# Moving the matmul operands of a two-layer decoder step to other byte offsets in SBUF

## The chip, the cores and the metric

The kernel runs on one core of one Trainium2 chip. The metric is the device time of one execution in microseconds (us). Before the change it is 2714.65 us, the median of three runs that lie between 2712.93 and 2714.92 us.

## The reference

One inference step of a decoder with two layers, for 256 prompt tokens and 64 sample tokens together (320 token columns), with 2048 model features and a hidden width of 8192. Layer 0 mixes tokens by gated linear attention, layer 1 by a spatial gate; both are followed by a dense MLP with a squared ReLU.

```python
def sq_relu_mlp(x, w1, w2):
    return jnp.square(jax.nn.relu(x @ w1)) @ w2
...
            if i % N_MIXERS == 0:
                h, s = gla_mixer(x, gla_w_in[j], gla_w_gate[j], gla_b_gate[j], gla_norm_g[j],
                                 gla_w_out[j], gla_state0[j])
...
                h, v_rows = sg_mixer(x, sg_w_in[j], sg_b_in[j], sg_v_norm_g[j], sg_v_norm_b[j],
                                     sg_w_spatial[j], sg_b_spatial[j], sg_w_out[j])
...
            x = layer_norm(DEEPNORM_ALPHA * x + h, ln1_g[i], ln1_b[i])
            x = layer_norm(DEEPNORM_ALPHA * x + sq_relu_mlp(x, mlp_w1[i], mlp_w2[i]), ln2_g[i], ln2_b[i])
```

Nearly all of the arithmetic lies in the dense products `x @ w` of these five weight matrices and the two MLPs.

## The kernel before

Activations lie transposed: 16 blocks of 128 features, each 128 partitions by 320 tokens in fp32. A product is made of *units*: 4 x 128 rows by 256 columns of a weight matrix, 512 KB, loaded by one DMA of the SP queue (`unit`, line 126). ScalarE rounds the raw weights to a high part `wh` in fp32r (line 139), and VectorE makes the low part `wl` as the difference (line 140). Activations are kept as a high and a low part in the same way (`xh`/`xl`, `yh`/`yl`, `hh`/`hl` and so on, made by `parts`). A product of full precision is then three matmuls, written by `mm3` (lines 150 to 152): low weights by high activations, high weights by low activations, high weights by high activations. We call these three a **triple**. Each of its matmuls has a weight block of 128x128 as the stationary operand, and 320 token columns as the moving one. A unit is 8 triples; 16 triples that run over the 16 feature blocks fill one tile of 128 output features in PSUM.

After a normalization the first two units' columns are multiplied from the un-normalized values, with two more columns for the scale and the shift (the width is TW = 322 there, tiles `dgh` and `dgl`), while the normalization runs beside it (`gemm_of`); there are three such places of 64 triples each. All the other triples are 320 wide.

The weight parts live in rings: a `Ring` is a pool tag for `wh` and one for `wl`, with four buffers each. In the first layer's mixer there is one ring (`a`), after it two (`a` and `b`) in turn, so that a buffer comes back after 4 units first and after 8 units later. Tile's scheduler sets the order of the instructions of each engine; buffers that come free release the splitting of the next weights.

What matters here are **addresses inside a partition**, taken modulo 256 bytes. In the built program before the change:

- `wh` starts at 0. A block inside it starts at a multiple of 512 bytes, so every high block is at 0. `Ring.part` puts a gap of 16 words between the two tags, so every `wl` block is at 64.
- `bigtile` starts an activation tile of 320 columns at `LINE // 2` = 32 words. A feature block is 1280 bytes, five times 256, so every moving operand of a 320-wide triple, high or low, is at 128.
- A block of 322 columns is 1288 bytes, so in the 322-wide triples the moving operand of feature block k is at 8 k, and goes from 0 to 120. High and low parts are at the same offset there.

So before the change each of the 320-wide triples has the same three pairs of offsets (moving, stationary): (128, 64), (128, 0), (128, 0).

Of the kernel before, what the change touches and what calls it, by code (L numbers as in the profile page):

```python
# [8 lines left out]
F32 = mybir.dt.float32  # L9
F32R = mybir.dt.float32r  # L10
# [5 lines left out]
P = 128  # L16
D = 2048
KT = D // P
TP = 256
DB, DS = 8, 8  # L20
T = TP + DB * DS
# [12 lines left out]
LINE = 64  # L34
BIG = KT * T + LINE


V_BG, V_NG = 0, 8
V_L1G, V_L1B, V_L2G, V_L2B = 24, 56, 88, 120
V_SB, V_SG, V_SBB = 152, 184, 200  # L40
# [3 lines left out]
class Ring:  # L44


    def __init__(self, pool, tag):
        self.pool, self.tag, self.gap = pool, tag, False

    def part(self, p, name):  # L50

        t = self.pool.tile([P, UK, UN], F32R, tag=p + self.tag, name=name)
        if not self.gap:
            self.pool.tile([P, LINE // 4], F32, tag="gap", name=name + "_gap", bufs=1)
            self.gap = True
        return t


# [18 lines left out]
def step_kernel(ctx: ExitStack, tc: tile.TileContext, A):  # L77
# [3 lines left out]
    def nm(s):  # L81
        uid[0] += 1
        return f"{s}_{uid[0]}"
# [2 lines left out]
    cp = ctx.enter_context(tc.tile_pool(name="cp", bufs=1))  # L86
    big = ctx.enter_context(tc.tile_pool(name="big", bufs=1))
    wraw = ctx.enter_context(tc.tile_pool(name="wraw", bufs=3))
    wa = ctx.enter_context(tc.tile_pool(name="wa", bufs=4))
    mm = ctx.enter_context(tc.tile_pool(name="mm", bufs=4, space=bass.MemoryType.PSUM))  # L90
    gls = ExitStack()
    gl = gls.enter_context(tc.tile_pool(name="gl", bufs=4, space=bass.MemoryType.PSUM))
    mx = None

    rings = [Ring(wa, "a")]
    turn = [0]
    banks = [0]
    units = [0]
# [25 lines left out]
    def col(c):  # L124
        return vec[:, c : c + 1]
# [28 lines left out]
    def group(w, row0, cols, rh, rl, evict, side=None, width=T, before=None):  # L154

        ps = [mmtile(width) for _ in range(2 * len(cols))]
        for q in range(NU):
            if before is not None:
                before(q)
            for i, c in enumerate(cols):  # L160
                wh, wl = unit(w, row0, q, c, next_ring())
                for n in range(2):
                    for kk in range(UK):
                        k = q * UK + kk
                        mm3(ps[2 * i + n][:], wh, wl, kk, n, rh, rl, k, 0, width, k == 0, k == KT - 1)
                if side is not None:
                    side()
        for n in range(2 * len(cols)):
            evict(n, ps[n])
# [11 lines left out]
    lp = l2 = z = None  # L181
# [2 lines left out]
    w_in = A["gla_w_in"]  # L184
    C_Q, C_K, C_V, C_R = 0, H * DK, 2 * H * DK, 2 * H * DK + H * DV

    def bigtile(tag, dt, name, width=T):

        t = (lp if tag == "b1" else big).tile([P, BIG], dt, tag=tag, name=nm(name))
        start = LINE // 2 if width == T else 0
        return t[:, start : start + KT * width].rearrange("p (k t) -> p k t", t=width)

    def parts(pair, name, width=T):
        return bigtile(pair + "0", F32R, name + "h", width), bigtile(pair + "1", F32R, name + "l", width)

    xh, xl = parts("a", "x")
    o_all = bigtile("b0", F32, "o_all")  # L200

    gst = ExitStack()
# [104 lines left out]
    class Head:  # L307


        def __init__(hd, h):  # L310
            hd.h = h
            hd.eb, hd.ei, hd.ee = {}, {}, {}
# [304 lines left out]


    oh, ol = parts("a", "o")

    def split_o(ks):
        for k in ks:
            nc.scalar.copy(oh[:, k, 0:T], o_all[:, k, 0:T])
            nc.vector.tensor_sub(ol[:, k, 0:T], o_all[:, k, 0:T], oh[:, k, 0:T].bitcast(F32))

    def second_half():

        nonlocal lp, l2, z, gl, mx
        side.flush()
        split_o(range(4 * (H - 1), 4 * H))  # L630
        gst.close()
        gls.close()
        gl = ctx.enter_context(tc.tile_pool(name="gs", bufs=2, space=bass.MemoryType.PSUM))
        mx = ctx.enter_context(tc.tile_pool(name="mx", bufs=2, space=bass.MemoryType.PSUM))
        banks[0] = 3
        lp = ctx.enter_context(tc.tile_pool(name="lp", bufs=1))
        l2 = ctx.enter_context(tc.tile_pool(name="l2", bufs=2))
        wb = ctx.enter_context(tc.tile_pool(name="wb", bufs=4))
        rings.append(Ring(wb, "b"))
        wb.tile([P, LINE // 4], F32, tag="fill", name="fill_b", bufs=1)  # L640
        z = lp.tile([P, KT, T], F32, tag="z", name="z")
        lp.tile([P, 3 * LINE // 4], F32, tag="fill", name="fill_l")
        for q in range(2):
            nc.gpsimd.dma_start(z[:, 8 * q : 8 * q + 8, :], xT[:, 8 * q : 8 * q + 8, :])

# [112 lines left out]
    def gemm(w, row0, col0, rh, rl, evict, quad=False, side=None, before=None):  # L758

        i = 0  # L760
        while i < D // UN:
            n2 = 2 if quad and i == 0 else 1
            group(w, row0, [col0 + (i + m) * UN for m in range(n2)], rh, rl,
                  lambda n, ps, i=i: evict(2 * i + n, ps), side, before=before if i == 0 else None)
            i += n2

    def gemm_of(norm, out, w, col0, evict_raw, evict):

        yh, yl = parts(out, "y")
        norm.close()  # L770
        side = Side([lambda j=j: norm.apply(j, yh, yl) for j in range(KT)], 3 * NU)
        group(w, 0, (col0, col0 + UN), *norm.raw, evict_raw, side, width=TW)
        side.flush()
        for i in range(2, D // UN):
            group(w, 0, (col0 + i * UN,), yh, yl, lambda n, ps, i=i: evict(2 * i + n, ps))
        return yh, yl
# [23 lines left out]
    def mlp(i, norm, y_in, h_in, vg, vb, raw, last=False):  # L800

        w1, w2 = A["mlp_w1"][i], A["mlp_w2"][i]
        NC_ = 4
        for c in range(NC_):
            hs = []

            def sq_relu(j, x, r):
                if not hs:
                    hs.extend(parts(h_in, "h"))
                hh, hl = hs  # L810
                f = l2.tile([P, T], F32, tag="f", name=nm("f"))
                nc.vector.scalar_tensor_tensor(f[:], x, 0.0, r[:], op0=ALU.max, op1=ALU.mult)
                nc.scalar.copy(hh[:, j, 0:T], f[:])  # L813
                nc.vector.tensor_sub(hl[:, j, 0:T], f[:], hh[:, j, 0:T].bitcast(F32))  # L814

            def evict(j, ps):
                r = l2.tile([P, T], F32, tag="r", name=nm("r"))
                nc.scalar.activation(r[:], ps[:], AF.Relu)
                sq_relu(j, ps[:], r)

            def evict_raw(j, ps):
                t, wb_ = norm.correct(ps)
                r = l2.tile([P, T], F32, tag="r", name=nm("r"))
                nc.scalar.activation(r[:], t[:], AF.Relu, bias=wb_)
                sq_relu(j, r[:], r)

            if c == 0:
                yh, yl = gemm_of(norm, y_in, w1, 0, evict_raw, evict)
            else:
                gemm(w1, 0, c * D, yh, yl, evict)  # L830
            if c < NC_ - 1:
                def evz(j, ps, s=ALPHA if c == 0 else 1.0):
                    nc.vector.scalar_tensor_tensor(z[:, j, :], z[:, j, :], s, ps[:], op0=ALU.mult, op1=ALU.add)
                gemm(w2, c * D, 0, *hs, evz)
            else:
                return residual_gemm(w2, *hs, c * D, 1.0, vg, vb, raw, last=last)
# [4 lines left out]
    def before(q):  # L841
        if q == NU - 1:
            second_half()

    norm = residual_gemm(A["gla_w_out"], oh, ol, 0, ALPHA, V_L1G, V_L1B, "b", quad=True,
                         side=side, before=before)
    norm = mlp(0, norm, "a", "b", V_L2G, V_L2B, "a")


# [21 lines left out]
    def put_v(j, x, bias):  # L871
        nonlocal v, nv
        if j == 0:
            v = bigtile("a0", F32, "v")
            nv = Norm(v, V_SG, V_SBB)
        vj = v[:, j, 0:T]
        nc.scalar.activation(vj, x, AF.Gelu, bias=bias)
        if j >= KT // 2:
            nc.vector.tensor_sub(vj, vj, nv.c[:])
        nv.add(j)  # L880
        if j == 3:
            spatial()

    def ev_v_raw(j, ps):
# [2 lines left out]
        nc.vector.tensor_add(bias[:], wb_, col(V_SB + KT + j))  # L887
        put_v(j, t[:], bias[:])

    yh, yl = gemm_of(norm, "b", A["sg_w_in"], D, ev_v_raw, lambda j, ps: put_v(j, ps[:], col(V_SB + KT + j)))  # L890

    nv.close()
    oV = A["o_vT"].rearrange("(k p) t -> p k t", p=P)
# [39 lines left out]
        steps.append(lambda j=j: mixed(j, *mix(j)))  # L933
    side = Side(steps, 6 * NU)
    gemm(A["sg_w_in"], 0, 0, yh, yl, ev_u, side=side)
    ph, pl = parts("b", "p")
    for k in range(KT):
        nc.scalar.copy(ph[:, k, 0:T], v[:, k, 0:T])  # L938
        nc.vector.tensor_sub(pl[:, k, 0:T], v[:, k, 0:T], ph[:, k, 0:T].bitcast(F32))

    norm = residual_gemm(A["sg_w_out"], ph, pl, 0, ALPHA, V_L1G + KT, V_L1B + KT, "a", quad=True)
    norm = mlp(1, norm, "b", "a", V_L2G + KT, V_L2B + KT, "b", last=True)


    on_pool = (5, 9, 13)
    dh, dl = norm.raw
    ps = {}
# [17 lines left out]
    for j in range(KT):  # L965
        y, g, b = z[:, j, :], col(norm.vg + j), col(norm.vb + j)
# [79 lines left out]
```

## Time and profile before

| What | Value |
|---|---|
| median of three runs | 2714.65 us |
| the profiled execution: its own time | 2714.89 us |
| the profiled execution: its span, first to last instruction | 2713.2 us |
| granted TensorE clock, mean over the span | 0.999 |
| HBM read, written | 409.6 MB, 22.0 MB |
| share of the DMA engines' time in the queue of the weights | 47.8% |

The profile is one execution. Its own time is 1.7 us longer than its span, and 0.24 us longer than the median. In the rows that follow, a group is named by source line, engine, operation and by the program's tile names, out<-in. "PE" is a matmul and "PEld" a weight load; matmuls overlap in the pipeline, so that the duration of one is about twice the distance to the next one.

### The profile page before, as it was taken

Reading aid. Unit: us, or ns where it says so; the run is one execution under the profiler, and the core shown is the slowest. Engines: PE = TensorE matmul, PEld = TensorE weight load, DVE = VectorE, ACT = ScalarE, POOL = GpSimd, SP = SyncE. Lnnn points to the kernel's source line nnn. Section 1 sums busy time; section 2 is a strip of 40 time slices with the busy share of each in tenths; the row PEclk is TensorE's granted clock in tenths of the full one; section 3 lists DMA queues with packets and bytes.
Section 4 is the critical chain, followed back from the end, with each engine's and each line's share of the span. In section 5 each row is a group of like instructions: output and inputs, shape, how many; then the busy total and the mean of one; then the engine's idle time right before and its main releaser. Section 6 shows DMA issues by size and latency. Waiting matters only on the chain.

```text
span 2713.2 us, 44623 instructions
## 1 busy us (share of the span) xinstructions
PE 2692.2 (99%) x18493; PEld 2668.4 (98%) x18493; DVE 1543.0 (57%) x2284; ACT 1183.7 (44%) x1698; POOL 54.8 (2%) x84
## 2 busy tenths in 40 slices
PE   8999999999999999999999999999999999999998
PEld 8999999999999999999999999999999999999998
DVE  6577577885444444444468764687444444444456
ACT  5545455564334334333446554455334323333433
POOL 1000000000000000000000000000000000000001
PEclk9999999999999999999999999999999999999999
DMA  6557566645444444444445444454444445444542
GB/s 227 175 193 239 164 216 208 214 140 161 155 149 155 148 155 150 153 153 150 155 142 170 156 140 133 140 159 154 155 149 154 152 152 154 150 155 150 154 151 75
DMA packets 126395, 434.51 MB, mean 160 GB/s; under 512 B 13680, under 2 KB 17904, under 8 KB 126192
## 3 DMA queue, kind: packets, MB, share of 16 engines
q1 hardware_dynamic: 118800, 407.29, 47.8%
q0 software_dynamic: 6512, 23.20, 2.5%
q8 instruction: 144, 2.36, 0.3%
q10 hardware_dynamic: 880, 1.18, 0.1%
q14 instruction: 59, 0.48, 0.1%
HBM read 409.60 MB, written 22.02 MB: 159 GB/s over the span
## 4 chain that ended last, share of the span: by engine, by line
PE 98%; DVE 1%; ACT 0%; DMA 0%; issue 0%; SPq 0%; ACTq 0%; DVEq 0%
PE mm L150 32%; PE mm L152 31%; PE mm L151 31%; PE gl L565 1%; PE gl L568 1%; PE gl L523 1%; PE gl L905 0%; DMA xr<-xT 0%; PE gl L507 0%; ACT z L979 0%; DMA raw<-gla_w_in 0%; PE gl L900 0%; PE gl L508 0%; PE gl L432 0%; PE gl L434 0%
## 5 line engine op out<-in xcount | busy, mean ns | idle before, releaser
L140 DVE TENSOR_TENSOR wl<-raw,wh 128x1024 fp32r<-128x1024 f32 (+1 forms) x738 | 902.1, 1223 | 943.4 <-ACT wh L139 941.6
L139 ACT CAST wh<-raw 128x1024 fp32r<-128x1024 f32 (+1 forms) x738 | 772.1, 1048 | 1204.5 <-PE mm L152 1080.0
L152 PE MATMUL mm<-yh,wh 128*128 128x320 f32 x2368 | 726.4, 307 | 0.0
L150 PE MATMUL mm<-yh,wl 128*128 128x320 f32 x2368 | 724.3, 309 | 0.0
L151 PE MATMUL mm<-yl,wh 128*128 128x320 f32 x2368 | 716.7, 303 | 0.0
L150 PE MATMUL mm<-hh,wl 128*128 128x320 f32 x2048 | 630.8, 308 | 0.0
L152 PE MATMUL mm<-hh,wh 128*128 128x320 f32 x2048 | 628.7, 307 | 0.0
L151 PE MATMUL mm<-hl,wh 128*128 128x320 f32 x2048 | 619.6, 303 | 0.0
L151 PEld LDWEIGHTS mm<-yl,wh 128*128 128x128 f32 x2368 | 444.4, 188 | 0.0
L152 PEld LDWEIGHTS mm<-yh,wh 128*128 128x128 f32 x2368 | 442.9, 187 | 0.0
L150 PEld LDWEIGHTS mm<-yh,wl 128*128 128x128 f32 x2368 | 442.9, 188 | 0.0
L150 PEld LDWEIGHTS mm<-hh,wl 128*128 128x128 f32 x2048 | 384.4, 188 | 0.0
L151 PEld LDWEIGHTS mm<-hl,wh 128*128 128x128 f32 x2048 | 384.4, 188 | 0.0
L152 PEld LDWEIGHTS mm<-hh,wh 128*128 128x128 f32 x2048 | 383.0, 187 | 0.0
L150 PE MATMUL mm<-xh,wl 128*128 128x320 f32 x768 | 242.6, 316 | 10.2 <-ACT xh L216 5.7
L152 PE MATMUL mm<-xh,wh 128*128 128x320 f32 x768 | 238.0, 310 | 0.0
L151 PE MATMUL mm<-xl,wh 128*128 128x320 f32 x768 | 236.4, 308 | 0.0
L150 PEld LDWEIGHTS mm<-xh,wl 128*128 128x128 f32 x768 | 145.2, 189 | 15.0 <-ACT xh L216 5.7
L151 PEld LDWEIGHTS mm<-xl,wh 128*128 128x128 f32 x768 | 145.4, 189 | 3.6 <-issue 1.2
L152 PEld LDWEIGHTS mm<-xh,wh 128*128 128x128 f32 x768 | 145.1, 189 | 1.3
L150 PE MATMUL mm<-ph,wl 128*128 128x320 f32 x256 | 78.5, 308 | 1.0 <-ACT ph L938 1.0
L814 DVE TENSOR_TENSOR hl<-f,hh 128x320 fp32r<-128x320 f32 x128 | 62.3, 489 | 29.5 <-ACT hh L813 29.5
(271 smaller groups left out, 2482.7 us busy)
## 6 DMA issues: line engine op xcount, KB each, us to landing
raw<-mlp_w SPq DMA_DIRECT2D x512, 512.0 KB, 3.5
raw<-gla_w_in SPq DMA_DIRECT2D x94, 512.0 KB, 3.9
raw<-sg_w_in SPq DMA_DIRECT2D x64, 512.0 KB, 3.5
st<-state SPq DMA_DIRECT2D x32, 512.0 KB, 4.1
o_state_s<-st POOLq DMA_DIRECT2D x32, 512.0 KB, 3.8
raw<-gla_w_out SPq DMA_DIRECT2D x32, 512.0 KB, 4.3
raw<-sg_w_out SPq DMA_DIRECT2D x32, 512.0 KB, 3.5
z<-xT POOLq DMA_DIRECT2D x2, 1280.0 KB, 11.8
```

The costliest lines, as they stand in the source:

```text
L139: nc.scalar.copy(hi[:, ks, :], raw[:, ks, :])
L140: nc.vector.tensor_sub(lo[:, ks, :], raw[:, ks, :], hi[:, ks, :].bitcast(F32))
L150: nc.tensor.matmul(ps, wl[:, kk, s], x_h, start=first, stop=False)
L151: nc.tensor.matmul(ps, wh[:, kk, s], x_l, start=False, stop=False)
L152: nc.tensor.matmul(ps, wh[:, kk, s], x_h, start=False, stop=last)
L523: nc.tensor.matmul(pu[:], hd.ktp[:, blk, kt * P : (kt + 1) * P], hd.vtp[:, blk, :], start=(blk == 0), stop=(blk == 1))
L565: nc.tensor.matmul(po[:], qm[:, kt, b * P : (b + 1) * P], part[:], start=False, stop=(b == DB - 1 and kt == 1 and part is sth))
L568: nc.tensor.matmul(pu[:], kz[:, g, i, kt * P : (kt + 1) * P], hd.vts[:, g, :], start=True, stop=True)
L814: nc.vector.tensor_sub(hl[:, j, 0:T], f[:], hh[:, j, 0:T].bitcast(F32))
```

## The change

It changes no instruction and no size, only where tiles lie.

- Each ring has two buffers instead of four, and there are twice as many: `a` and `c` in the first layer's mixer, `b` and `d` as well after it, taken in turn. A buffer still comes back after 4 units, later after 8.
- The gap between the tags is now a ring's own, so `wl` blocks are at 128 (`a`), 192 (`c`), and 160 and 32 (the two rings that come later) modulo 256 in the built program; `wh` stays at 0. A quarter of the units, in the first layer's mixer half of them, has each offset.
- An activation tile starts at an offset of its own, from the table `PLACES` in words: twelve pairs (high, low) of multiples of 64 bytes. The first mixer's input and output have (0, 0); the MLPs' hidden parts, the inputs `y` and the spatial gate's product have one pair each. The 322-wide tiles start at 0 as before.
- `z` and the tiles behind it move by a few hundred bytes.

```diff
+PLACES = [[(0, 0), (16, 16), (32, 32), (48, 48), (0, 16), (16, 32)],
+          [(32, 48), (48, 0), (0, 48), (16, 0), (32, 16), (48, 32)]]
...
-    def __init__(self, pool, tag):
-        self.pool, self.tag, self.gap = pool, tag, False
+    def __init__(self, pool, tag, gap):
+        self.pool, self.tag, self.gap = pool, tag, [gap, LINE - gap]
...
-        if not self.gap:
-            self.pool.tile([P, LINE // 4], F32, tag="gap", name=name + "_gap", bufs=1)
-            self.gap = True
+        if self.gap:
+            self.pool.tile([P, self.gap.pop(0)], F32, tag=f"gap{p}{self.tag}", name=name + "_gap", bufs=1)
...
-    wa = ctx.enter_context(tc.tile_pool(name="wa", bufs=4))
+    wa = ctx.enter_context(tc.tile_pool(name="wa", bufs=2))
...
-    rings = [Ring(wa, "a")]
+    rings = [Ring(wa, "a", 32), Ring(wa, "c", 48)]
...
-    def bigtile(tag, dt, name, width=T):
+    def bigtile(tag, dt, name, width=T, start=0):
...
-        start = LINE // 2 if width == T else 0
...
-    def parts(pair, name, width=T):
-        return bigtile(pair + "0", F32R, name + "h", width), bigtile(pair + "1", F32R, name + "l", width)
+    def parts(pair, name, width=T, starts=(0, 0)):
+        return (bigtile(pair + "0", F32R, name + "h", width, starts[0]),
+                bigtile(pair + "1", F32R, name + "l", width, starts[1]))
...
-        wb = ctx.enter_context(tc.tile_pool(name="wb", bufs=4))
-        rings.append(Ring(wb, "b"))
+        wb = ctx.enter_context(tc.tile_pool(name="wb", bufs=2))
+        rings.extend((Ring(wb, "b", 8), Ring(wb, "d", 40)))
...
-        lp.tile([P, 3 * LINE // 4], F32, tag="fill", name="fill_l")
+        lp.tile([P, LINE], F32, tag="fill", name="fill_l")
...
-                    hs.extend(parts(h_in, "h"))
+                    hs.extend(parts(h_in, "h", starts=PLACES[i][c]))
...
-                yh, yl = gemm_of(norm, y_in, w1, 0, evict_raw, evict)
+                yh, yl = gemm_of(norm, y_in, w1, 0, evict_raw, evict, PLACES[i][4])
...
+    yh, yl = gemm_of(norm, "b", A["sg_w_in"], D, ev_v_raw, lambda j, ps: put_v(j, ps[:], col(V_SB + KT + j)),
+                     PLACES[0][5])
...
-    ph, pl = parts("b", "p")
+    ph, pl = parts("b", "p", starts=PLACES[1][5])
```

The scheduler answers to the other rings with a few moved instructions: none on SP and POOL, and on the other engines at the changeover from the first mixer to the first MLP, at the first columns of both MLPs, and at those of the spatial gate. Two of these places follow, each before and after the change.

On ScalarE, at the end of the first layer's mixer, where `wh` are the weight roundings of coming units, `os`, `o_all`, `sq` and `ny` finish the last head, and `oh` is the rounded input of the output product. Before:

```order
L577 COPY os_4851<-gl_4356 128x512
L139 CAST wh_5095<-raw_5094 128x1024
L583 COPY o_all_91<-gl_4853 128x4x64
L586 ACTIVATE sq_4860<-o_all_91 128x256
L139 CAST wh_5173<-raw_5172 128x1024
L139 CAST wh_5064<-raw_5063 128x1024
L139 CAST wh_5143<-raw_5142 128x1024
L175 ACT_TABLE_LOAD
L175 ACTIVATE ny_4867<-gl_4863,eps_h 128x320
```

The same place after the change:

```order
L576 COPY os_4854<-gl_4359 128x512
L582 COPY o_all_91<-gl_4856 128x4x64
L141 CAST wh_5147<-raw_5146 128x1024
L141 CAST wh_5099<-raw_5098 128x1024
L585 ACTIVATE sq_4863<-o_all_91 128x256
L141 CAST wh_5067<-raw_5066 128x1024
L141 CAST wh_5177<-raw_5176 128x1024
L141 CAST wh_5209<-raw_5208 128x1024
L177 ACT_TABLE_LOAD
L177 ACTIVATE ny_4870<-gl_4866,eps_h 128x320
```

One copy of the head moved ahead of a rounding, and one more rounding stands ahead of the root's table load.

On VectorE, in the first columns of the first MLP, where `wl` are the weights' low parts, `yl` and `t` belong to the normalization that runs beside the matmuls, and `f` and `hl` make the hidden activations. Before:

```order
L814 TENSOR_TENSOR hl_6355<-f_6378,hh_6354 128x320
L140 TENSOR_TENSOR wl_6779<-raw_6777,wh_6778 128x1024
L747 TENSOR_TENSOR yl_6017<-z,yh_6016 128x320
L742 SCALAR_TENSOR_TENSOR t_6405<-t_6405,vec,rstd_6020 128x320
L814 TENSOR_TENSOR hl_6355<-f_6389,hh_6354 128x320
L742 SCALAR_TENSOR_TENSOR t_6411<-t_6411,vec,rstd_6020 128x320
L140 TENSOR_TENSOR wl_6883<-raw_6881,wh_6882 128x1024
```

And after the change:

```order
L813 TENSOR_TENSOR hl_6361<-f_6384,hh_6360 128x320
L746 TENSOR_TENSOR yl_6023<-z,yh_6022 128x320
L741 SCALAR_TENSOR_TENSOR t_6411<-t_6411,vec,rstd_6026 128x320
L813 TENSOR_TENSOR hl_6361<-f_6395,hh_6360 128x320
L741 SCALAR_TENSOR_TENSOR t_6417<-t_6417,vec,rstd_6026 128x320
L142 TENSOR_TENSOR wl_6859<-raw_6857,wh_6858 128x1024
L142 TENSOR_TENSOR wl_6889<-raw_6887,wh_6888 128x1024
```

One low part of a unit (`wl_6779`, which is `wl_6785` in the changed program) is made some nine rows later than before.

More of the change, by code (lines that the diff above doesn't have):

```diff
@@ L765, in gemm, with gemm_of @@
             i += n2
-    def gemm_of(norm, out, w, col0, evict_raw, evict):
-        yh, yl = parts(out, "y")
+    def gemm_of(norm, out, w, col0, evict_raw, evict, starts):
+        yh, yl = parts(out, "y", starts=starts)
         norm.close()
@@ L888, in ev_v_raw @@
         put_v(j, t[:], bias[:])
-    yh, yl = gemm_of(norm, "b", A["sg_w_in"], D, ev_v_raw, lambda j, ps: put_v(j, ps[:], col(V_SB + KT + j)))
+    yh, yl = gemm_of(norm, "b", A["sg_w_in"], D, ev_v_raw, lambda j, ps: put_v(j, ps[:], col(V_SB + KT + j)),
+                     PLACES[0][5])
     nv.close()
```

## The prediction

> **What bounds the kernel now.** I read the page from the top, then the waits of TensorE, then its groups by shape, and last single matmuls in order of time.
>
> ```profile
> PE 2692.2 (99%) x18493; PEld 2668.4 (98%) x18493; DVE 1543.0 (57%) x2284; ACT 1183.7 (44%) x1698; POOL 54.8 (2%) x84
> PEclk9999999999999999999999999999999999999999
> ```
>
> ```profile
> PE mm L150 <- ACT xh L216: 5.7, 1, 5.7
> PE mm L150 <- DVE wl L140: 2.2, 2, 1.6
> PE mm L150 <- DVE qd L411: 2.2, 1, 2.2
> ```
>
> ```profile
> ACT wh L139 <- PE mm L152: 1080.0, 488, 3.7
> ```
>
> TensorE is at work in 99% of the span at the full clock, and its largest waits sum to 10 us, more than half of it before the first matmul. It is the other way round: the rounding of the weights waits 1080 us in all for matmuls to give buffers back. So weights are ready long before they are used, and the time is the number of matmuls times the distance from one to the next. The counts:
>
> ```profile
> L152 PE MATMUL mm<-yh,wh 128*128 128x320 f32 x2368 | 726.4, 307 | 0.0
> L150 PE MATMUL mm<-yh,wl 128*128 128x320 f32 x2368 | 724.3, 309 | 0.0
> L151 PE MATMUL mm<-yl,wh 128*128 128x320 f32 x2368 | 716.7, 303 | 0.0
> L150 PE MATMUL mm<-hh,wl 128*128 128x320 f32 x2048 | 630.8, 308 | 0.0
> ...
> L150 PE MATMUL mm<-xh,wl 128*128 128x320 f32 x768 | 242.6, 316 | 10.2 <-ACT xh L216 5.7 <-DVE wl L140 2.2 <-DVE qd L411 2.2
> ...
> L150 PE MATMUL mm<-ph,wl 128*128 128x320 f32 x256 | 78.5, 308 | 1.0 <-ACT ph L938 1.0
> L150 PE MATMUL mm<-oh,wl 128*128 128x320 f32 x256 | 77.8, 308 | 0.6 <-DVE nw L176 0.6
> ```
>
> Line 150 stands once in a triple: 2368 + 2048 + 768 + 256 + 256 = 5696 triples of 320 columns. Three stretches far inside the MLPs, with the number of matmuls in the first bracket, give their pace:
>
> ```profile
> 700.00:810.00 110.00, 110.00 (x764) 110.00 (x763) 47.20 (x50) 34.73 (x36) 0.00 (x0) 1.00 0.49 153
> 900.00:1010.00 110.00, 110.00 (x763) 110.00 (x762) 46.16 (x49) 33.59 (x32) 0.00 (x0) 1.00 0.47 154
> 1200.00:1310.00 110.00, 110.00 (x763) 110.00 (x763) 50.75 (x58) 40.83 (x52) 0.00 (x0) 1.00 0.48 151
> ```
>
> A matmul that began up to 0.31 us ahead of the stretch counts in it, so 2290 matmuls take 330.9 us: 144.5 ns each, **433.5 ns a triple**. All 320-wide triples come to 5696 x 0.4335 = 2469 us, 91% of the span.
>
> Is that the pace at which columns stream through? Ahead of 9 us the clock is still at half:
>
> ```profile
> 7.54 0.47 PE L151 MATMUL mm<-xl,wh 128*128 128x320 f32 x1
> 7.81 0.47 PE L152 MATMUL mm<-xh,wh 128*128 128x320 f32 x1
> 8.08 0.47 PE L151 MATMUL mm<-xl,wh 128*128 128x320 f32 x1
> 8.35 0.47 PE L152 MATMUL mm<-xh,wh 128*128 128x320 f32 x1
> ```
>
> Here a matmul takes 0.81/3 = 270 ns at the most. At the full clock the columns alone would then need about half, 135 ns, or 0.42 ns a column; the triple's 433.5 ns have some 28 ns on top. The three lines of a triple also differ though all are 320 columns: their mean durations are 309, 303 and 307. The end of a matmul is modelled; with the mean distance of 144.5 against the mean duration of 306.3, 162 ns of a duration overlap the next, so the distances are about 147, 141 and 145 ns. Something of 6 to 12 ns a matmul depends on the operands. What differs between the lines is whose block moves and which weights are loaded meanwhile (PEld is busy 98%, so a load runs under every matmul). This is the part that addresses could touch.
>
> **The change, part by part.** It adds, removes and resizes no instruction. Three parts:
>
> *Rings of two.* A buffer comes back after 4 and 8 units as before, SP issues its DMAs in the same order, so the depth of the prefetch is kept. The scheduler's moves (a weight's low part made some nine VectorE rows later) cost nothing as long as splitting waits for matmuls, the 1080 us above; if that cover went, it would be a wait like the 1.6 us of the second row of waits, at some five places: 8 us at the most. I take 0.
>
> *The 322-wide triples.* Their moving offsets stay; only `wl` moves. 192 of 5888 triples, 0.
>
> *The 320-wide triples.* No triple keeps its offsets, and all 5696 get others: 5696 ns of span for each nanosecond of a triple. The trace has three places with other offsets.
>
> (a) The gate's product: moving operands at 128 as in the triples, the same 320 columns, but stationary ones at 224:
>
> ```profile
> 20.78 0.31 PE L292 MATMUL gl<-xl,wgp 128*128 128x320 f32 x1
> 20.92 0.31 PE L293 MATMUL gl<-xh,wgp 128*128 128x320 f32 x1
> ...
> 22.98 0.31 PE L293 MATMUL gl<-xh,wgp 128*128 128x320 f32 x1
> 23.12 0.31 PE L150 MATMUL mm<-xh,wl 128*128 128x320 f32 x1
> ```
>
> 16 matmuls in 2.34 us: 146.3 ns, or 438.8 for three, **+5.3 ns** a triple.
>
> (b) The 322-wide triples, at sixteen moving offsets from 0 to 120:
>
> ```profile
> 562.75 0.30 PE L150 MATMUL mm<-dgh,wl 128*128 128x322 f32 x1
> ...
> 577.47 0.31 PE L150 MATMUL mm<-dgh,wl 128*128 128x322 f32 x1
> 577.62 0.30 PE L151 MATMUL mm<-dgl,wh 128*128 128x322 f32 x1
> 577.76 0.31 PE L152 MATMUL mm<-dgh,wh 128*128 128x322 f32 x1
> 577.91 0.31 PE L150 MATMUL mm<-dgh,wl 128*128 128x322 f32 x1
> ...
> 578.36 0.31 PE L150 MATMUL mm<-dgh,wl 128*128 128x322 f32 x1
> ...
> 591.71 0.31 PE L150 MATMUL mm<-yh,wl 128*128 128x320 f32 x1
> ```
>
> 64 triples and four 320-wide matmuls of a sum (some 146 ns each, 0.58 us) in 28.96 us: 443.4 ns a triple. Six columns more than a 320-wide triple are 2.5 ns, so 440.9 at 320: **+7.4 ns**. The slowest of them, feature block 9, goes from 577.91 to 578.36: 450, less 2.5, is 14 ns above.
>
> (c) Block 8 there has the moving operands at 64, a multiple of 64 like all of the changed kernel's: 577.47 to 577.91 is 440, less 2.5, **+4**. The rows round to 10 ns, so this is no more than a sign.
>
> Below zero: nothing bars a better set of offsets, since the columns alone need 405 ns. The nearest row is line 151 at about 141 ns; three such are 424 ns, -9.5.
>
> All three places lie above 433.5, the best stretches of the trace are the ones with the old offsets, and the scatter between offsets (-9.5 to +14) averages out over 4 x 12 combinations. I take (a), the nearest in shape and the one between the other two: 5696 x 5.3 ns = +30.2 us. The profiled execution took 2714.9 us (0.24 us over the median of the runs, nothing at this size), so **2745 us**.
>
> A page speaks against any change at all. The Trainium skill, "TensorE: Matmul & The Clock Gate", Part 2 (What happens when you issue a matmul), says that TensorE has two independent read ports, one for the moving operand and one for the weights, and: "Loading the next tile's weights doesn't steal SBUF read bandwidth from the running matmul." By that rule no address matters and the time stays, which is the first of the rivals below. The trace does not agree: the matmuls above take 141 to 147 ns at one width.
>
> **The rivals.**
>
> *No effect.* What differs between the lines could be the sequence of operands, not their addresses: line 150 follows a change of weights, line 152 repeats them. Then the time is 2715, give or take 5. For it: lines 150 and 151 have the same offsets, moving 128 and next weights at 0, yet differ by 6 ns. Against it: (a) repeats its weights every second matmul and is slower, not faster, and (b) has the triple's very sequence.
>
> *Faster: the weights move out of the way.* Before, low and high weights lie 64 apart, now mostly 128 and more, and high and low activations no longer coincide in eight of the twelve pairs. If line 150's 147 ns come from a meeting of its stream with the load of `wh`, and the new distances avoid it so that all lines run as line 151, a triple takes 424 and the span loses 54 us; with half of the combinations so, 27 us: 2688. It decides from the point where the mean over the combinations falls under 432.5, which is 0.2%. Against it: none of the places with other offsets is under 433.5.
>
> *Half of the rings.* If offsets that are multiples of 64 are all alike, the rings with `wl` at 128 and 192 keep 433.5, and only those at 160 and 32 pay. They hold half of the triples after the first mixer, about 2390: x 5.3 is 13 us, 2728. For it: (a) stands at 224, which is no multiple of 64. Against it: block 8 in (b), and the pace is slow in that place through and through.
>
> *The bad end.* The new offsets behave as the worse half of (b), +10 ns: +57 us, 2772.
>
> **How the numbers follow.** A measurement of this kernel tells about 0.2% (5.4 us) from no change. Forecast, +3.5 to +8 ns a triple (2735 to 2761): 0.60. Half of the rings: 0.13, the bad end 0.07. No effect 0.11, faster 0.09. So slower has 0.60 + 0.13 + 0.07 = 0.80, same 0.11, faster 0.09. The range goes from 2714, through the half-rings case and the upper part of no effect, to 2764; outside are faster (0.09), the lower part of no effect (0.05) and most of the bad end (0.06).
>
> **What would show it.** In the changed profile the number of matmuls per 110 us falls from 763 to about 754, at the full clock and with no new waits of TensorE. The mean durations of lines 150 to 152 should rise by about 2 ns each and differ from one MLP chunk to the next (each chunk has its own pair) and from unit to unit (four low offsets). The first mixer, at pair (0, 0), should be slower too. If its pace stays and the MLPs' changes, half of the rings is right. Waits of TensorE for `wl` of many us would mean that the rings' depth, which I cost at nothing, was the matter. If (a) and (b) were slow for their own sake, short sequences that never settle, and every steady sequence settles near 433.5 at any offset, the forecast is wrong at its root.

## The result, and the profile after

The changed kernel takes 2754.01 us, the median of four runs (2752.70 to 2755.28), against 2714.78 us before (four runs, 2712.93 to 2714.93): 39.2 us longer, a ratio of 1.0146 with a 95% interval of 1.0133 to 1.0158. The forecast was 2745 us with a range of 2714 to 2764, and slower.

The first lines of the changed kernel's page, with the busy time of each engine, and the granted clock:

```profile
span 2753.3 us, 44617 instructions
...
PE 2728.7 (99%) x18493; PEld 2705.0 (98%) x18493; DVE 1546.0 (56%) x2284; ACT 1185.3 (43%) x1698; POOL 54.6 (2%) x84
...
PEclk9999999999999999999999999999999999999999
```

The same work, a granted clock of 0.9 or more in each of the 40 slices, and TensorE is still busy in 99% of a span that is 40.1 us longer. The waits of TensorE in the changed kernel:

```profile
PE mm L152 <- ACT xh L215: 5.6, 1, 5.6
PE mm L152 <- DVE nw L178: 4.8, 1, 4.8
PE mm L152 <- DVE wl L142: 2.3, 2, 1.7
```

One has grown: the wait put down to `nw` is 4.8 us instead of 0.6. It ends at 478.27 us, and behind it TensorE runs slowly. A stretch of 3 us before the change; the third number from the end is the granted clock, the first bracket the number of matmuls:

```profile
478.00:481.00 3.00, 3.00 (x23) 3.00 (x22) 3.00 (x6) 2.24 (x5) 1.54 (x2) 1.00 0.75 188
```

And after:

```profile
478.00:481.00 3.00, 2.73 (x10) 2.73 (x11) 2.31 (x4) 2.05 (x2) 0.00 (x0) 0.50 0.93 359
```

The clock is at half from 476.6 to 483.4 us. 19 matmuls take the 5.1 us from 478.27 on; at the 146 ns of full clock they would take 2.8, so the half clock costs an estimated 2.4 us more. The rest, some 33 us, must lie in the distance between matmuls at full clock. The stretches of 110 us shown of before, in the changed kernel; the bracket behind the first busy time is the number of matmuls:

```profile
700.00:810.00 110.00, 110.00 (x754) 110.00 (x753) 44.75 (x47) 33.63 (x32) 0.00 (x0) 1.00 0.49 151
900.00:1010.00 110.00, 110.00 (x756) 110.00 (x756) 46.10 (x50) 35.17 (x36) 0.00 (x0) 1.00 0.49 151
1200.00:1310.00 110.00, 110.00 (x751) 110.00 (x751) 49.47 (x56) 39.14 (x48) 0.00 (x0) 1.00 0.49 151
```

751 to 756 instead of 763 or 764. The page's groups (the last number before the second bar is the mean duration in ns):

```profile
L154 PE MATMUL mm<-yh,wh 128*128 128x320 f32 x2368 | 731.9, 310 | 0.0
L153 PE MATMUL mm<-yl,wh 128*128 128x320 f32 x2368 | 730.5, 309 | 0.0
L152 PE MATMUL mm<-yh,wl 128*128 128x320 f32 x2368 | 726.3, 309 | 0.0
L154 PE MATMUL mm<-hh,wh 128*128 128x320 f32 x2048 | 632.5, 309 | 0.0
L153 PE MATMUL mm<-hl,wh 128*128 128x320 f32 x2048 | 632.4, 309 | 0.0
L152 PE MATMUL mm<-hh,wl 128*128 128x320 f32 x2048 | 631.4, 308 | 0.0
```

Before, the three lines of a triple were at 309, 303 and 307. Line 153 (before: 151) has lost its 6 ns of advantage, line 154 some 2, line 152 nothing: the three lines are alike now.

For a closer look, the distance from the end of each matmul to the end of the next was taken from the trace, averaged over the units of a stage with one low offset (the outermost twentieth at either end left out), and summed over the three lines. This gives ns a triple for each combination. The first four columns are the changed kernel's, the last is from the experiment with the old rings below, where the low weights are at 64 throughout.

| (high, low) activations | low weights at 192 | 128 | 160 | 32 | 64 |
|---|---|---|---|---|---|
| (0, 0) | 438.6 | 435.8 | 440.3 | 440.4 | 440.0 |
| (64, 64) | 438.3 | 436.7 | 440.0 | 433.9 | 435.6 |
| (128, 128) | 440.2 | 440.0 | 439.7 | 440.2 | **433.4** (the kernel before) |
| (192, 192) | 440.0 | 436.8 | 437.6 | 443.3 | 440.0 |
| (0, 64) | 438.5 | 442.2 | 441.6 | 440.4 | 438.5 |
| (64, 128) | 439.7 | 439.7 | 442.2 | 440.0 | 438.8 |
| (192, 128) | 441.6 | 438.7 | 443.2 | 440.6 | 449.5 |
| (128, 64) | 436.6 | 443.4 | 442.9 | 438.2 | 436.7 |
| (128, 192) | 440.7 | 440.0 | 439.9 | 439.9 | 440.0 |
| (192, 0) | 441.8 | 433.5 | 434.2 | 439.9 | 440.0 |
| (0, 192) | 446.9 | 440.3 | 443.3 | 444.2 | 440.0 |
| (64, 0) | 445.6 | 438.0 | 446.7 | 440.2 | 439.9 |

Of these sixty, none is under 433.4, the value of the kernel before. 24 lie within 0.5 ns of 440, 19 below that and 17 above it.

### The profile page after: what moved, and what is told of

The parts are those of the page before. It is cut to its first block, busy times and chain, and to the rows that moved or that the text cites. A ratio compares the mean times of both kernels' runs of the same rounds, so it can differ in the third digit from the quotient of the medians.

```text
span 2753.3 us, 44617 instructions
## 1 busy us (share of the span) xinstructions
PE 2728.7 (99%) x18493; PEld 2705.0 (98%) x18493; DVE 1546.0 (56%) x2284; ACT 1185.3 (43%) x1698; POOL 54.6 (2%) x84
## 4 chain that ended last, share of the span: by engine, by line
PE 97%; DVE 1%; DMA 1%; ACT 1%; issue 0%; SPq 0%; ACTq 0%; DVEq 0%
PE mm L154 31%; PE mm L152 31%; PE mm L153 31%; PE gl L564 1%; PE gl L567 1%; PE gl L522 0%; PE gl L905 0%; PE gl L506 0%; DMA xr<-xT 0%; DMA raw<-gla_w_out 0%; DMA raw<-gla_w_in 0%; ACT z L979 0%; PE gl L900 0%; ACT wh L141 0%; DVE wl L142 0%
## 5 line engine op out<-in xcount | busy, mean ns | idle before, releaser
L153 PE MATMUL mm<-yl,wh 128*128 128x320 f32 x2368 | 730.5, 309 | 0.0
L153 PE MATMUL mm<-hl,wh 128*128 128x320 f32 x2048 | 632.4, 309 | 0.0
L152 PE MATMUL mm<-oh,wl 128*128 128x320 f32 x256 | 79.2, 313 | 4.8 <-DVE nw L178 4.8
L153 PE MATMUL mm<-ol,wh 128*128 128x320 f32 x256 | 79.8, 313 | 0.0
```

The lines of the kernel that those rows point to most:

```text
L152: nc.tensor.matmul(ps, wl[:, kk, s], x_h, start=first, stop=False)
L153: nc.tensor.matmul(ps, wh[:, kk, s], x_l, start=False, stop=False)
```

## The experiments

Theory A: the offsets modulo 256 set the distance between matmuls, and the old set is one of the few good ones. Theory B: the time comes from the rings of two or from the instructions that moved with them.

**Old offsets in the new rings.** The changed kernel with every offset put back:

```diff
-PLACES = [[(0, 0), (16, 16), (32, 32), (48, 48), (0, 16), (16, 32)],
-          [(32, 48), (48, 0), (0, 48), (16, 0), (32, 16), (48, 32)]]
+PLACES = [[(32, 32)] * 6, [(32, 32)] * 6]
-    rings = [Ring(wa, "a", 32), Ring(wa, "c", 48)]
+    rings = [Ring(wa, "a", 16), Ring(wa, "c", 16)]
-        rings.extend((Ring(wb, "b", 8), Ring(wb, "d", 40)))
+        rings.extend((Ring(wb, "b", 16), Ring(wb, "d", 16)))
```

> The changed kernel with its four rings of two and its order of instructions, but every offset put back: low weights at 64, all 320-wide activations at 128. Theory A (the offsets set the distance between matmuls): a triple is back at 433.5 ns, about 763 matmuls per 110 us; only the 4 to 5 us that TensorE waits more for the last head's root in the changed trace (4.8 us against 0.6) stay, so 2719 us. Theory B (rings of two or the moved instructions cost the time): 2754 us, 440 ns a triple.

Measured: 2719.71 us against 2714.33, a ratio of 1.0020 (1.0011 to 1.0030). Its stretches and its wait:

```profile
700.00:810.00 110.00, 110.00 (x764) 110.00 (x763) 46.95 (x50) 34.96 (x36) 0.00 (x0) 1.00 0.49 153
900.00:1010.00 110.00, 110.00 (x764) 110.00 (x763) 46.66 (x50) 35.16 (x36) 0.00 (x0) 1.00 0.50 153
```

```profile
PE mm L151 <- DVE nw L177: 4.9, 1, 4.9
```

The pace is back, the wait is not, and the half clock behind it is there too (0.50 between 478 and 481 us). So 5.4 us of the change belong to the rings, and 2754.0 - 2719.7 = 34.3 us to the offsets. Theory B falls but for these 5.4 us.

**The activations' offsets alone.** The kernel before with its rings of four and its low weights at 64, but with `PLACES` for the activations.

> The kernel before, with its rings of four and low weights at 64, but activations at the twelve pairs of offsets. Theory A: the stage that has the pair (128, 128) keeps 433.5 ns a triple, the others go to 436 to 444, about 439 in the mean: 2715 + 5440 x 5.5 ns = 2745 us, without the longer wait for the root. Theory B: 2715 us, 433.5 everywhere.

Measured: 2743.83 us, a ratio of 1.0107 (1.0092 to 1.0122). The stretches lie in the second products of the first MLP with the pairs (0, 0), (64, 64), (128, 128) and (192, 192), and in the output product of the spatial gate with (192, 128):

```profile
685.00:785.00 100.00, 100.00 (x684) 100.00 (x683) 41.74 (x43) 29.47 (x29) 0.00 (x0) 1.00 0.50 152
908.00:1008.00 100.00, 100.00 (x691) 100.00 (x690) 41.47 (x45) 30.43 (x29) 0.00 (x0) 1.00 0.50 152
1130.00:1230.00 100.00, 100.00 (x694) 100.00 (x693) 42.26 (x45) 30.60 (x31) 0.00 (x0) 1.00 0.48 152
1355.00:1455.00 100.00, 100.00 (x684) 100.00 (x683) 66.66 (x107) 42.29 (x59) 0.00 (x0) 1.00 0.49 149
1715.00:1815.00 100.00, 100.00 (x669) 100.00 (x668) 68.24 (x109) 41.93 (x60) 0.00 (x0) 1.00 0.49 153
```

Same code, same shapes, other places: 694 matmuls in 100.3 us are 433.6 ns a triple, 691 are 435.5, 684 are 440.0 and 669 are 449.8. The stage with the old pair kept the old pace, as theory A expected. In 8 of the 14 stages the table's method gives 439.9 or 440.0.

**The low weights' offsets alone.** The changed kernel with all 320-wide activations back at 128 (`PLACES` all (32, 32)), low weights at 192, 128, 160 and 32.

> The changed kernel with all 320-wide activations back at 128, low weights still at 192, 128, 160 and 32. Theory A: all four low offsets stand at 440 ns with the pair (128, 128) in the changed trace, so 2715 + 5696 x 6.5 ns + 4 us = 2756 us, no better than with the twelve pairs: moving the low weights alone is enough to lose the pace. If instead the activations' offsets did it: 2719 us.

Measured: 2753.85 us, a ratio of 1.0144 (1.0128 to 1.0159), as slow as the whole change. All four offsets stand at 439.3 to 440.5 ns inside the MLPs, multiples of 64 and others alike. That ends the rival "half of the rings": 128 and 192 lose the old pace just as 160 and 32 do. Either half of the change alone is enough to lose it, and the two losses do not add.

**Everything 64 bytes further.** The kernel before with a pad of 16 words ahead of the weights, and activations 16 words further:

```diff
+    wa.tile([P, 16], F32, tag="pad", name="pad", bufs=1)
     rings = [Ring(wa, "a")]
...
-        start = LINE // 2 if width == T else 0
+        start = (LINE // 2 if width == T else 0) + (0 if tag == "b1" else 16)
```

The tile `b1` lies behind the pad and moves with it, so all 320-wide activations come to 192, high weights to 64 and low ones to 128.

> The kernel before with every weight and activation tile 64 bytes further: high weights at 64, low at 128, activations at 192, so that all distances between operands are kept. If only distances between operands count: 433.5 ns a triple, 2715 us. If the places themselves count: about 440 ns and 2745 to 2752 us.

Measured: 2715.04 us, a ratio of 0.9999 (0.9989 to 1.0008), and 433.4 ns a triple. Between this and the old set only the common place differs, so for a shift of 64 it is the distances between the operands that count.

**Worst pair everywhere.** The kernel before with all 320-wide activations at (192, 128).

> The kernel before, low weights at 64, but every 320-wide activation at the pair (192, 128), which stood at 449.5 ns a triple in the run with the old rings and the new activations. If the distance between matmuls belongs to the offsets and to nothing of the stage: 2714.7 + 5696 x 16.1 ns = 2806 us, the pace about 734 matmuls per 110 us in every stage. If that stage was slow for another reason (its activations come out of the spatial gate): about 2750 us, 440 ns.

Measured in one run: 2797.69 us, beside 2715.46 for the kernel before: 82 us or 3.0% from offsets alone. Two stretches in the MLPs:

```profile
700.00:800.00 100.00, 100.00 (x669) 100.00 (x668) 40.17 (x42) 29.05 (x28) 0.00 (x0) 1.00 0.47 144
...
2000.00:2100.00 100.00, 100.00 (x669) 100.00 (x668) 40.43 (x42) 29.73 (x31) 0.00 (x0) 1.00 0.48 145
```

449.8 ns there, so the stage was not the reason. The time is 8 us under the expectation because five of the 14 stages, the first mixer among them, stand at 445 to 447: the same offsets can settle into more than one rhythm.

**Order of a triple, half loads, fewer columns.** The kernel before, with the second products of the MLPs altered one by one; in the second MLP their activations are at (0, 0).

```diff
+        if mode[0] == 1:
+            nc.tensor.matmul(ps, wh[:, kk, s], x_h, start=False, stop=False)
+            nc.tensor.matmul(ps, wh[:, kk, s], x_l, start=False, stop=last)
...
+            if mode[0] == 2:
+                nc.tensor.matmul(ps[0:64, :], wh[:, kk, n * P : n * P + 64], x_l, start=False, stop=False)
+            elif mode[0] == 3:
+                nc.tensor.matmul(ps[:, 0:TP], wh[:, kk, s], x_l[:, 0:TP], start=False, stop=False)
```

> The kernel before (low weights at 64, 320-wide activations at 128), with three of the four second products of each MLP altered; in the second MLP their activations are at 0, a pair that stands at 440.0 ns a triple. First product: the last two matmuls of a triple change places. Second product: the matmul of high weights by low activations loads and multiplies only 64 of the 128 columns of its block, so half of that term is left out. Third product: the same matmul streams only 256 of its 320 columns, so that term is left out for the sample tokens. Theory C, from the 440.0 ns that most pairs share: 440 ns is 3 x 352 cycles of 2.4 GHz, 32 more than columns, and a load of 128 columns is 32 lines of 16 bytes; each line loaded costs the matmul that streams meanwhile one cycle, lucky offsets save some. It expects at (0, 0): second product 433.3 ns a triple, with line L (low weights), under which the halved load runs, at 140.0 and the others at 146.7; third product 413.3, the shortened matmul at 120.0. If the cost is a tenth of the columns streamed: second 440.0, third 410.7 with 117.3. If it is one of each matmul: second 440.0, third 413.3. First product at (128, 128): if offsets and loads alone count, 433.4, with 147, 142, 144.5 in their old places; if the operands count (low activations quick), the 142 moves to the third place. Whole time about 2700 us.

Measured in one run: 2707.27 us. First the order, at (128, 128): the groups of a stretch from 690 to 770 us, with the last two matmuls exchanged (line 155 is now high by high, line 156 high by low):

```profile
L153 PE MATMUL mm<-hh,wl 128*128 128x320 f32 x186 | 57.3, 308 | 0.0
L156 PE MATMUL mm<-hl,wh 128*128 128x320 f32 x185 | 56.8, 307 | 0.0
L155 PE MATMUL mm<-hh,wh 128*128 128x320 f32 x185 | 56.0, 303 | 0.0
```

The quick matmul is still the second of the three: the 303 ns went over to high by high. So it is not the moving part, high or low activations, that makes the difference. The order of the weights (low, high, high) is the same in both, and this exchange does not test it. Then the second and third products in both MLPs, half load and 256 columns at (128, 128), and the same at (0, 0):

```profile
900.00:1000.00 100.00, 100.00 (x684) 97.33 (x683) 41.53 (x43) 29.83 (x29) 0.00 (x0) 1.00 0.48 152
1120.00:1220.00 100.00, 100.00 (x740) 100.00 (x739) 45.00 (x47) 32.60 (x32) 0.00 (x0) 1.00 0.51 163
...
2135.00:2235.00 100.00, 100.00 (x691) 97.60 (x690) 42.10 (x44) 30.20 (x30) 0.00 (x0) 1.00 0.47 150
2357.00:2457.00 100.00, 100.00 (x728) 100.00 (x727) 44.18 (x46) 32.11 (x32) 0.00 (x0) 1.00 0.51 162
```

With 64 columns less to stream a triple takes 406.7 ns (740 matmuls) and 413.4 (728), 26.7 and 26.6 less than 433.4 and 440.0. That is 0.417 ns for each of the 64 columns, and the half-clock rows of the prediction gave 0.42 for a column alone. A cost in proportion to the columns falls. With half a load the triple at (0, 0) goes from 440.0 to 435.5, where theory C expected 433.3, and line 153 in it is at 144.6 by the trace instead of 140.0; at (128, 128) it goes *up*, from 433.4 to 440. That speaks against theory C, and for a second test. The whole time is 7 us above the 2700 that was expected.

**Narrow loads in all three matmuls.**

```diff
+        m = {1: 64, 2: 32}.get(mode[0], P)
+        if m < P and not first and not last:
+            s, ps = slice(n * P, n * P + m), ps[0:m, :]
```

> The kernel before, with the first two second products of each MLP altered: from the second to the last but one feature block, all three matmuls of a triple load and multiply only 64 (first product) or 32 (second) of the 128 columns of their weight block, so the other rows of these sums are left out. Activations of the second products at 128 in the first MLP, at 0 in the second. If each 16-byte line loaded costs the streaming matmul one cycle (theory C): at (0, 0) 16 and 8 cycles over the 320, 140.0 and 136.7 ns a matmul, 420 and 410 ns a triple; at (128, 128) no more than that. If the cost is one of each matmul whatever it loads (32 cycles): 146.7 and 440 in both. The half load of one matmul in the run before gave 435.4 and 440.0, which fits neither of the two well. Whole time by theory C: 1024 triples less by about 17 to 30 ns in the mean, some 2690 to 2700 us.

Measured in one run: 2723.26 us, where theory C gave 2690 to 2700. Loads of 64 and of 32 columns at (128, 128), and the same at (0, 0):

```profile
680.00:780.00 100.00, 100.00 (x688) 92.96 (x687) 41.63 (x43) 29.36 (x28) 0.00 (x0) 1.00 0.48 152
900.00:1000.00 100.00, 100.00 (x685) 77.36 (x684) 41.80 (x44) 29.44 (x28) 0.00 (x0) 1.00 0.48 148
...
1925.00:2025.00 100.00, 100.00 (x687) 92.97 (x686) 40.50 (x42) 30.24 (x29) 0.00 (x0) 1.00 0.49 150
2145.00:2245.00 100.00, 100.00 (x688) 77.38 (x687) 41.07 (x44) 30.43 (x29) 0.00 (x0) 1.00 0.50 152
```

The second busy time, of the weight loads, falls to 93 and 77 us of 100, so the loads did get shorter; the matmuls hardly came closer. 685 to 688 are 437 to 439 ns a triple: 2 to 3 ns less than the 440.0 of full loads at (0, 0), and 4 to 6 more than their 433.4 at (128, 128). Theory C, with 410 to 420 at (0, 0), falls: what is paid over the columns is about 13 ns of each matmul (as long as 32 columns), whether 32 or 128 columns are loaded under it.

**Two scans for a better set.** The changed kernel with low weights at 64, 96, 32 and 224 and pairs in steps of 16 bytes:

> The changed kernel with other offsets: low weights at 64, 96, 32 and 224, and twelve pairs of activation offsets in steps of 16 bytes. Theory C: most combinations of pair and low offset near 440.0 ns a triple (32 cycles a matmul), a few below it and a few above, the mean between 438 and 441; whole time 2745 to 2758 us. A rival by which only multiples of 64 are good or bad alike would put steps of 16 at one value of their own, above 443. Whether any combination lies clearly under 433.4 is open; I expect one in fifty.

Measured in one run: 2754.29 us, mean 440.3 ns a triple. And with further pairs and weight offsets, where the built program has the weights (high, low) at (0, 64), (32, 96), (32, 160) and (64, 160), and none of the low ones at the 0 that the expectation names:

> As the run with steps of 16 bytes, with other offsets of the weights (high ones at 0, 32 and 64 in turn, low ones at 0, 64 and 160) and twelve more pairs of activations, among them (0, 128), (128, 0), (64, 192) and (192, 64), which the changed kernel leaves out. Theory C: mean 438 to 441 ns a triple, 2745 to 2758 us; the four left-out pairs no different from the others.

Measured in one run: 2758.41 us, 0.4 above the expected range, mean 440.5. Steps of 16 bytes are no worse than steps of 64, and three of the pairs that the changed kernel leaves out, (0, 128), (64, 192) and (192, 64), stand between 440 and 445. The fourth, (128, 0), was not met: some tiles lay 32 bytes off the plan in this run, and it fell on (128, 32), at 440 to 447. The lowest combination of both scans is 433.8 (pair (80, 80), low weights at 224), so none is under the kernel before; the highest is 453.1 (pair (208, 208), low weights at 64). With nothing better found, no version that beats both kernels was there to run.

## Why the prediction was right

*What bounds the kernel.* Right. The time is the number of matmuls times their distance: the offsets' 34.3 us over 5696 triples are 6.0 ns a triple. No part of it is a wait.

*The price of other offsets.* The term was +5.3 ns, from place (a), the gate's product, between (b) with +7.4 and (c) with +4. Measured are 6.0, or 34.3 us where 30.2 were forecast. Of the 9 us by which the forecast fell short, 4 are this term and 5 the rings. Place (a) read 438.8 over 16 matmuls, while the mean of the 48 combinations is 440.1; that one place with one stationary offset came so near is in part luck, since single combinations lie anywhere from 433.5 to 446.9. The argument that carried was that three places with unrelated offsets all lay above the old set, and that 48 combinations would average to what is common, not to what is best. The range of single combinations, -9.5 to +14, was somewhat short above (+16 at the worst pair of the table, +20 in a scan) and too generous below: in some 150 combinations nothing is under 433.4.

*The rings, costed at nothing.* Here a step was mis-sized: 5.4 us, inside the 8 us named as the price without cover, but not at the place that the working looked at (the late low part in the MLP). It was the other place with moved rows, at the end of the first mixer, and not a wait for weights. ScalarE and VectorE there in the changed kernel, and what TensorE waited for:

```profile
467.98 2.36 DVE L142 TENSOR_TENSOR wl<-raw,wh 128x1024 fp32r<-128x1024 f32 x2 [1.95 <-ACT wh L141]
...
470.79 1.93 DVE L470 SCALAR_TENSOR_TENSOR o_all<-o_all,vec,sr 128x320 f32<-128x320 f32 x4
...
472.80 3.05 ACT L141 CAST wh<-raw 128x1024 fp32r<-128x1024 f32 x3 [3.58 <-issue]
...
473.87 3.50 DVE L142 TENSOR_TENSOR wl<-raw,wh 128x1024 fp32r<-128x1024 f32 x3 [1.16 <-ACT wh L141]
475.87 1.28 ACT L177 ACT_TABLE_LOAD   x1
477.16 0.53 ACT L177 ACTIVATE ny<-gl,eps_h 128x320 f32<-128x320 f32 x1
477.72 0.49 DVE L178 TENSOR_SCALAR nw<-gl 128x320 f32<-128x320 f32 x1 [0.35 <-ACT ny L177]
...
478.27 0.64 PE L152 MATMUL mm<-oh,wl 128*128 128x320 f32 x1 [4.84 <-DVE nw L178]
```

The same place before:

```profile
465.85 1.47 DVE L471 SCALAR_TENSOR_TENSOR o_all<-o_all,vec,sr 128x320 f32<-128x320 f32 x3
...
466.92 2.96 ACT L139 CAST wh<-raw 128x1024 fp32r<-128x1024 f32 x3 [2.11 <-DMA raw<-gla_w_out]
...
469.90 1.28 ACT L175 ACT_TABLE_LOAD   x1
...
471.19 0.53 ACT L175 ACTIVATE ny<-gl,eps_h 128x320 f32<-128x320 f32 x1
...
471.75 0.49 DVE L176 TENSOR_SCALAR nw<-gl 128x320 f32<-128x320 f32 x1 [0.24 <-ACT ny L175]
...
472.30 0.41 PE L150 MATMUL mm<-oh,wl 128*128 128x320 f32 x1 [0.58 <-DVE nw L176]
```

In both kernels TensorE starts when `nw`, the first VectorE row of the last head's root, has ended. The low parts ahead of it had ended too, at 477.37 in the changed kernel, so weights were not what was missing. The root came late because ScalarE stood still for 3.6 us ahead of three roundings that precede it. The view names no releaser, but the trace holds ScalarE's wait instruction for the first of them: it stands from 467.32 to 472.75, until the last of the four `o_all` rows on VectorE has ended at 472.72. Before, the wait for the same unit's rounding took 0.1 us, since these rows ended at 467.32. They came later (the changed kernel as a whole was some 1.6 us behind here) because two roundings now precede the last head's squares (`sq`) on ScalarE, and the two low parts at 467.98 precede the sum of these squares on VectorE. The 1080 us in which splitting waits for matmuls are a sum over the kernel; at this one place the cover was thin before, as the 0.6 us of wait showed. The half clock behind the wait was no term of the working at all.

*No effect.* It had the sequence of operands as the reason for the difference between lines. The exchanged order speaks against the moving parts as that reason, and the changed kernel against the order of the weights alone: the order is the same there, and the lines stand at 309, 309 and 310. The Trainium skill's rule ("TensorE: Matmul & The Clock Gate", Part 2: the load of the next weights takes no read bandwidth from the running matmul) is not refuted in its wording, since triples with loads of 32 columns stand at 437 to 439 ns, between the 433.4 and 440.0 with loads of 128. What was drawn from it, that no address matters, is: 34 us come from addresses.

*Faster*, *half of the rings*, *the bad end*. The first decides under 432.5 in the mean, and 440.1 was measured. The second fell with the low weights alone (its 2390 triples were 2440 in the built program, and its 13 us stay). The third exists, as 449.5 at one pair, but needs one bad pair throughout.

*The signs.* 754 matmuls per 110 us were named, 751 to 756 came. The mean durations rose by 0, 6 and 2 ns, not by 2 each. No new waits was another sign, and it failed: one wait grew by 4.2 us. The first mixer was to be slower too; it is, by little: between 100 and 210 us 732 matmuls stand against 734. Its low weights are at 192 and 128, where the pair (0, 0) stands at 438.6 and 435.8 in the table; by the same method its triples take 438.8 and 436.7 ns, against 435.3 before.

What stays open is the cause of the 13 ns and of the exceptions. It is no share of the columns and no price of the loaded columns, it depends on distances between moving and stationary offsets, and its sum over a triple likes to settle at 40 ns over the columns' 400.

## What to carry to other kernels

Where matmuls run back to back, look at the distances between them and not only at waits: here 3% of the time hangs on where operands lie modulo 256 bytes, with all engines' work unchanged. A tuned set of offsets is a combination; here moving either operand alone lost it, and a common shift of 64 bytes kept it. And a change of pools that only renames buffers can still move a few instructions at a place where the cover is thin, so look there for waits that are already above zero, and at the granted clock behind them.

## What the runs showed that was not expected

- A triple of 320-wide matmuls settles at 440.0 ns for very different offsets (8 of 14 stages of one run), 146.7 ns a matmul, 13.3 above the columns at 0.417 ns each. The best sets reach 433.4 to 433.9, and nothing in some 150 combinations less. A mean can hide a rhythm of unequal triples.
- Cutting the loaded weight columns from 128 to 32 left 437 to 439 ns, and at the good offsets made it slower than the full load (433.4): a shorter load can cost time.
- The same offsets can run in more than one rhythm: (192, 128) with low weights at 64 stood at 450 ns in most stages and at 445 to 447 in others of one run. The 450 are triples of 447 and 453 ns in turn. In the spatial gate's output product in the run with the old rings, 61 of the slow ones fall on even feature blocks and 62 on odd ones, so the block's own address does not decide which is slow.
- A longer wait cost more than its own time: in all five runs in which TensorE waited 3.9 to 5.0 us for `nw`, the granted clock then fell to half for 3.4 or 6.8 us, and in the six with 0.8 us or less it did not.
